# The last four head tiles of branch A in the written order, and merge rows loaded one merge ahead

## The chip, the cores and the metric

The kernel runs on one core of a Trainium2 chip. The core has a matrix engine (TensorE, PE in the profile, with PEld for the loading of its stationary operand), a vector engine (VectorE, DVE), a scalar engine (ScalarE, ACT), a general one (GpSimd, POOL) and a queue that mostly issues transfers (SyncE, SP). Each works through its own instructions in order and waits on semaphores for the others. The metric is the device time of one execution in microseconds (us); less is better.

## The reference, cut to what matters

One encoder layer over 1280 rows (1024 of a sample, 256 of a prompt), width 1024, with two attention branches, gates, an MLP and a final norm:

```python
z = rmsnorm(x, g_mix) @ w_in                 # q, k, v of both branches, and 2 x 1024 gate columns
gates = sigmoid(z[..., o6:] + b_gate)
o_a = banded_attention(qa, ka, va, 128, 1, bias_a, sink)     # 8 heads of 64
o_b = dilated_mixture(qb, kb, vb, bias_b)    # three groups of 4 heads; softmax over the groups' lse
merged = gates[0] * (o_a @ w_branch_a) + gates[1] * (o_b @ w_branch_b)
x = x + merged @ w_out
y = rmsnorm(x + square(relu(rmsnorm(x, g_mlp) @ w_up)) @ w_down, g_final)
```

Matrix products are made from two parts of each operand, a high and a low half (`hi` and `lo`), with three matmuls per product.

## The kernel before, in words

The layer is worked off in stages: input projection and branch B's attention (up to about 600 us), branch A's heads (600 to 768), the branch products with the gates (768 to 860), then `merged @ w_out` and the MLP. The change is in the heads and the branch products.

**The heads.** Branch A has 40 head tiles: four units (two heads each) of ten row tiles. Tile i goes through three steps, in three successive rounds of a loop: `scores` (L1016 to L1024: four score matmuls into two `sc` banks, on DVE a reduction per head, L1018, which also adds the bias, then `nm_a`, L1022, the exponentials on ACT, L1024), `transposes` (L1039: four or six 128x128 transposes on PE into `pt` banks, and their copies), `values_of` (L1053: the value matmuls, a copy, a store to `scr_o`). After each step stands `tick(n)`, n = 0 to 125, which puts other work between: fill and merges.

- Fill is `logits()`: five weight chunks of gate columns times all rows, in 45 steps of eight matmuls (L192), six of them ahead of the loop; `done[0] * 122 < 39 * n` places the others. Their results are stored to `scr_g` (L1076).
- A merge (L1078 to L1122) takes rows of branch B's three groups from `scr_b`, in a tile `r` (loads L1086 to L1097), weighs them by the softmax of their lse on DVE and ACT (L1102 is its first DVE instruction) and leaves `merged`. There are ten, of four steps each, from n = 32 on. The loads are the merge's first step, its arithmetic the next.
- `turn_merged(t)` turns two 128x128 blocks of `merged` on PE (L1137) into one `pt` bank; `split` then writes the high half on ACT (`obhi`, L185) and the low half on DVE (`oblo`, L186), per block.

The bank pools: three `mm`, two `sc`, two `pt`, one `pv`. A `pt` bank is used by a head tile's transposes, by `turn_merged` and by `turn_a`, and comes free when its readers are done.

**The branch products.** 48 jobs of one 128-column chunk and one block of rows each; for the first block eight of branch B (six matmuls), then four of branch A (twelve). A job's product is multiplied by its gate (L1262, L1264) into `mT`. Gates are loaded from `scr_g` (L1222) and opened with the sigmoid (L1227), five and two jobs ahead. A table `side` says before which jobs `turn_a` and `turn_merged` run. `turn_a(t)` divides a row tile of branch A's output by its sum (L1155, DVE), turns its four blocks (L1158, PE) and splits them (`ohi`, `olo`). Weights pass through `fetch` (the load, L222) and `prepare` (`whi` on ACT, L231, `wlo` on DVE, L235).

**What sets the order.** The stages up to 600 us, and from the second half of `w_out` on, are issued in the order in which they are written (`tc.manual_schedule`). In the heads and the branch products a scheduler decides the order of each engine's instructions from the written program.

Of the kernel before, what the change touches and what calls it, by code (L numbers as in the profile page):

```python
# [10 lines left out]
F32 = mybir.dt.float32  # L11
# [4 lines left out]
P = 128  # L16
# [81 lines left out]
def encoder_kernel(  # L98
# [31 lines left out]
    def wslot(name, shape=(P, D), dt=F32):  # L130
        return slots.tile(list(shape), dt, name=name, tag="w", bufs=N_W)
# [52 lines left out]
    def split(hi, lo, src):  # L184
        nc.scalar.activation(hi, src, AF.Copy)  # L185
        nc.vector.tensor_tensor(lo, src, hi.bitcast(F32), op=ALU.subtract)  # L186
# [199 lines left out]
    def then(*gens):  # L386
        for g in gens:
            yield from g
# [604 lines left out]
    if True:  # L993
# [84 lines left out]
        def merge(i, t):  # L1078

            r = wslot("r", (P, 2, 3, ROW))
# [16 lines left out]
            yield  # L1099
            nm, ls = r[:, :, :, 2 * HD : 2 * HD + 2], r[:, :, :, 2 * HD + 2 :]  # L1100
            mm = small.tile([P, 2, 2], F32, name="mm_", tag="m")
            nc.vector.tensor_tensor(mm, nm[:, :, 0], nm[:, :, 1], op=ALU.min)  # L1102
# [20 lines left out]
            yield  # L1123


    mT = Wide("mT", KC, F32, ())
    if True:
        ob_hi, ob_lo = Wide("obhi", 2, F32R, ()), Wide("oblo", 2, F32R, ())
        o_hi, o_lo = Wide("ohi", 4, F32R, ()), Wide("olo", 4, F32R, ())

        def turn_merged(t):
            if t in (0, 4, 8):
                ob_hi.block(t // 4)
                ob_lo.block(t // 4)
            ps = bank("pt")
            for j in range(2):
                nc.tensor.transpose(ps[:, P * j : P * j + P], merged[t // 4][:, t % 4, P * j : P * j + P], ident)  # L1137
            k = 8 if t < 8 else 2
            for j in range(2):
                hi, lo = (x.at(j, P * t, P).rearrange("p (q m) -> p q m", m=k) for x in (ob_hi, ob_lo))  # L1140
                split(hi, lo, ps[:, P * j : P * j + P].rearrange("p (m q) -> p q m", m=k))

        rows_o = {}

        def load_o(t):
            rows_o[t] = slot("o", (P, AH, HD))
            nc.sync.dma_start(rows_o[t], scr_o[t].rearrange("p (h d) -> p h d", h=AH))

        def turn_a(t):
# [5 lines left out]
            nc.vector.tensor_tensor(o, o, l_a[:, :, t].unsqueeze(2).to_broadcast([P, AH, HD]), op=ALU.mult)  # L1155
            ps = bank("pt")
            for k in range(4):
                nc.tensor.transpose(ps[:, P * k : P * k + P],  # L1158
                                    o[:, 2 * k : 2 * k + 2, :].rearrange("p h d -> p (h d)"), ident)
            p3 = ps.rearrange("p (k q) -> p k q", k=4)  # L1160
            per = o_hi.per(P * t)
            for k in range(0, 4, per):
                split(o_hi.at(k, P * t, P, per), o_lo.at(k, P * t, P, per), p3[:, k : k + per, :])
# [5 lines left out]
        merges = then(*[merge(i, t) for t in range(0, NT, 2) for i in range(2)])  # L1169
        done = [0, 0]  # L1170

        def tick(n):
# [12 lines left out]
            while done[1] * 80 < 40 * (n - 32):  # L1185
                next(merges, None)
                done[1] += 1

        steps_of(fill, 6)
        for i in range(len(order) + 2):  # L1190
            if i < len(order):
                u, t = order[i]
                if t == 0 and u < 3:
                    units[u + 1] = load_unit(u + 1), load_bias(u + 1, lambda name, shape: a3(name, shape, 2))
                scores(u, t)
                tick(3 * i)
# [11 lines left out]
        w_as = [weight(0), weight(0), None, None]  # L1208

        jobs = [(x, b, c) for b in range(3) for x in "ba" for c in range(KC if x == "b" else 4)]  # L1210
        jobs += [("a", b, c) for b in range(3) for c in range(4, KC)]
# [14 lines left out]
                c = jobs[i][2] + KC * (jobs[i][0] == "b")  # L1226
                nc.scalar.activation(sgs[i], sgs[i], AF.Sigmoid, bias=bg[:, c : c + 1])  # L1227

        for i in range(5):
            load_gate(i)  # L1230
        open_gate(0)
        open_gate(1)
        side = {0: (turn_a, 0), 2: (turn_merged, 4), 3: (turn_a, 1), 4: (turn_merged, 5), 5: (turn_a, 2),
                6: (turn_merged, 6), 7: (turn_a, 3), 9: (turn_merged, 7), 12: (turn_a, 4), 14: (turn_a, 5),
                16: (turn_a, 6), 18: (turn_a, 7), 20: (turn_merged, 8), 22: (turn_merged, 9), 26: (turn_a, 8),
                30: (turn_a, 9)}
        for i, (x, b, c) in enumerate(jobs):
            t0, n = BLOCKS[b]
            load_gate(i + 5)
            open_gate(i + 2)  # L1240
            if i in side:
                f, t = side[i]
                f(t)
                if f is turn_a and t + 4 < NT:
                    load_o(t + 4)
            if i in (24, 28):
# [494 lines left out]
```

## Time and profile before

| | us |
|---|---|
| runs | 1784.59, 1785.34, 1787.38 |
| median | 1785.34 |
| profiled execution: time | 1786.2 |
| profiled execution: span | 1784.4 |
| PE busy in the span | 1729.1 (97%) |
| DVE, ACT, POOL busy | 988.8, 716.3, 502.1 |

How to read the profile's lines. A timeline row gives the start and the length in us, the engine, the line of the kernel, the operation, output<-inputs, its shape, how many like it, and in brackets the engine's idle time before it with what released it. A row of a group gives the count, then the busy time, the mean in ns, and the idle time before it. A row of waits gives the waiting engine and line, what it waited for, then total, times and the longest. "fp32r" is the type of the split halves. The clock (PEclk) is the share of its full speed that TensorE was granted.

### The profile page before, as it was taken

What the parts mean: (1) busy time and instruction counts of PE and PEld (TensorE: products, weight loads), DVE (VectorE), ACT (ScalarE), POOL (GpSimd) and SP (SyncE); (2) the same over time, 40 slices, a digit from 0 to 9 for tenths busy, and PEclk for the clock granted to TensorE, in tenths of its full rate; (3) what the DMA queues carried; (4) which work ended last, traced back from release to release, by engine and by line L of the source; (5) the groups of instructions that cost most, each with busy time, mean ns of one, the idle gap of its engine ahead of it and who ended that gap; (6) DMA issues with size and microseconds to landing.
All of it is one profiled execution on the core that took longest, in us unless ns stands there. A gap on an engine that the chain in (4) does not pass through costs nothing.

```text
span 1784.4 us, 25203 instructions
## 1 busy us (share of the span) xinstructions
PE 1729.1 (97%) x9248; PEld 1464.8 (82%) x9248; DVE 988.8 (55%) x1683; ACT 716.3 (40%) x1533; POOL 502.1 (28%) x396
## 2 busy tenths in 40 slices
PE   7999999999999999899999799999999999999998
PEld 6898888777777899878888688888888788888886
DVE  6623333355545357676647655454554875667575
ACT  6232223344444354465336433333333433333345
POOL 0222321223222111100010345455555451315050
PEclk9999999999999999999999899999999999999999
DMA  6415335555454833454411144433445854623333
GB/s 231 144 38 165 108 105 148 141 149 147 138 160 144 289 110 100 142 207 158 158 44 80 57 129 151 150 122 125 130 151 175 300 200 144 237 98 121 120 112 118
DMA packets 218067, 256.26 MB, mean 144 GB/s; under 512 B 21455, under 2 KB 148771, under 8 KB 217816
## 3 DMA queue, kind: packets, MB, share of 16 engines
q1 hardware_dynamic: 209512, 232.32, 40.2%
q0 software_dynamic: 7344, 20.24, 3.4%
q10 hardware_dynamic: 1088, 2.10, 0.3%
q8 instruction: 73, 1.20, 0.3%
q14 instruction: 50, 0.41, 0.1%
HBM read 169.10 MB, written 90.73 MB: 146 GB/s over the span
## 4 chain that ended last, share of the span: by engine, by line
PE 61%; DVE 4%; ACT 2%; issue 1%; DMA 1%; SPq 0%; POOL 0%; DVEq 0%; ACTq 0%; POOLq 0%
PE dn L344 20%; PE mm L192 13%; PE x L344 10%; PE pv L344 5%; PE z L344 4%; PE y L344 2%; PE pv L1053 2%; PE pt L1039 1%; PE sc L1016 1%; PE sc L1017 1%; PE mm L344 1%; DVE ulo L186 0%; PE pv L538 0%; DMA scr_u<-u 0%; DVE clo L311 0%
## 5 line engine op out<-in xcount | busy, mean ns | idle before, releaser
L344 PE MATMUL x<-chi,wlo 128*128 128x512 f32 x424 | 171.8, 405 | 6.9 <-ACT phi L185 6.9
L344 PE MATMUL dn<-dhi,ulo 128*128 128x512 f32 x448 | 174.6, 390 | 2.6 <-DVE ulo L186 2.6
L344 PE MATMUL dn<-dhi,uhi 128*128 128x512 f32 x448 | 174.3, 389 | 0.0
L344 PE MATMUL dn<-dlo,uhi 128*128 128x512 f32 x448 | 174.3, 389 | 0.0
L344 PE MATMUL x<-clo,whi 128*128 128x512 f32 x424 | 168.3, 397 | 0.0
L344 PE MATMUL x<-chi,whi 128*128 128x512 f32 x424 | 167.8, 396 | 0.0
L377 POOL TENSOR_TENSOR tb<-raw 128x512 f32<-128x512 f32 x30 | 40.1, 1338 | 442.6 <-PE mm L192 130.0
L311 DVE TENSOR_TENSOR wlo<-ta,whi 128x1024 fp32r<-128x1024 f32 x30 | 55.9, 1864 | 186.3 <-ACT whi L309 171.7
L311 DVE TENSOR_TENSOR wlo<-raw,whi 128x1024 fp32r<-128x1024 f32 x60 | 92.2, 1537 | 106.5 <-ACT whi L309 106.5
L344 PEld LDWEIGHTS dn<-dhi,ulo 128*128 128x128 f32 x448 | 84.1, 188 | 20.9 <-DVE ulo L186 3.6
L344 PEld LDWEIGHTS x<-chi,wlo 128*128 128x128 f32 x424 | 81.7, 193 | 22.9 <-ACT phi L185 7.3
L344 PEld LDWEIGHTS dn<-dhi,uhi 128*128 128x128 f32 x448 | 84.1, 188 | 17.6
L186 DVE TENSOR_TENSOR ulo<-uraw,uhi 128x1024 fp32r<-128x1024 f32 x56 | 91.9, 1662 | 11.7 <-ACT uhi L185 11.7
L344 PEld LDWEIGHTS dn<-dlo,uhi 128*128 128x128 f32 x448 | 84.1, 188 | 17.3
L344 PEld LDWEIGHTS x<-chi,whi 128*128 128x128 f32 x424 | 81.3, 192 | 18.0
L515 ACT ACTIVATE s<-s,o 128x128 f32<-128x128 f32 (+1 forms) x120 | 52.4, 437 | 102.8 <-DVE o L513 55.0
L344 PEld LDWEIGHTS x<-clo,whi 128*128 128x128 f32 x424 | 81.7, 193 | 14.4
L1458 POOL TENSOR_TENSOR t<-raw,t 128x1024 f32<-128x1024 f32 x16 | 47.2, 2969 | 142.5 <-DMA raw<-in_w_down_dram 138.4
L1609 DVE TENSOR_TENSOR v<-v,dn 128x512 f32<-128x512 f32 x90 | 59.5, 682 | 42.5 <-PE dn L344 38.2
L344 PE MATMUL dn<-dhi,up 128*128 128x512 f32 x224 | 73.5, 389 | 0.0
L344 PE MATMUL pv<-phi,wlo 128*128 128x256 f32 x256 | 72.4, 283 | 0.9 <-ACT u L1629 0.9
L344 PE MATMUL z<-chi,wlo 128*128 128x512 f32 x184 | 72.6, 395 | 0.0
(327 smaller groups left out, 4753.2 us busy)
## 6 DMA issues: line engine op xcount, KB each, us to landing
scr_u<-u SPq DMA_DIRECT2D x112, 320.0 KB
uraw<-scr_u SPq DMA_DIRECT2D x56, 512.0 KB
raw<-in_w_in_dram SPq DMA_DIRECT2D x33, 512.0 KB
raw<-in_w_up_dram SPq DMA_DIRECT2D x32, 512.0 KB
raw<-in_w_down_dram SPq DMA_DIRECT2D x28, 512.0 KB
sg<-scr_g SPq DMA_DIRECT2D x32, 256.0 KB
uraw<-scr_u SPq DMA_DIRECT2D x28, 256.0 KB
v<-scr_v SPq DMA_DIRECT2D x96, 64.0 KB
```

Of the source, the lines that this page charges most:

```text
L186: nc.vector.tensor_tensor(lo, src, hi.bitcast(F32), op=ALU.subtract)
L192: nc.tensor.matmul(ps, a, b, start=i == 0, stop=i == len(seq) - 1)
L311: nc.vector.tensor_tensor(lo, src, hi.bitcast(F32), op=ALU.subtract)
L344: nc.tensor.matmul(ps, a, b, start=first and i == 0, stop=last and i == len(seq) - 1, skip_group_check=True)
L377: nc.gpsimd.tensor_tensor(tb[:, 0], b12, b11, op=ALU.subtract)
L515: nc.scalar.activation(s[:, h, :W], s[:, h, :W], AF.Exp, bias=nm[:, h : h + 1], accum_out=l[:, h : h + 1])
L1016: nc.tensor.matmul(ps[:, :W], q, st["k"][1][:, P * lo : P * lo + W], start=True, stop=False)
L1017: nc.tensor.matmul(ps[:, :W], q, st["k"][0][:, P * lo : P * lo + W], start=False, stop=True)
L1039: nc.tensor.transpose(ps[:, P * (i % 4) : P * (i % 4) + P], s[:, h, P * b : P * b + P], ident)
L1053: nc.tensor.matmul(pv[:, HD * h : HD * h + HD], pt[:, 2 * b + h, :], src, start=b == 0, stop=b == W // P - 1)
L1458: nc.gpsimd.tensor_tensor(o, a, b, op=ALU.subtract)
L1609: nc.vector.tensor_tensor(v, v, ps, op=ALU.add)
```

## The change

1. A merge's rows are loaded one merge ahead (`load_rows`, `merges_of`): the loads of the first merge go out before its first step, and those of merge n + 1 ahead of the arithmetic of merge n. Merges begin at n = 6 in place of 32 and run at 41 steps per 96 in place of 40 per 80.
2. Fill runs at 31 steps per 120 in place of 39 per 122, and stops at 31 of the 39. Of the eight left, four run in the last two rounds of the loop, which have no scores, three or four among the divisions of the first row tiles, and the rest behind them.
3. From tile 36 until job 40 the written order holds (`last.enter_context(tc.manual_schedule(engines=ALL))` to `last.close()`).
4. `turn_merged` 0 to 3 stand at the beginning of rounds 36 to 39. The turn leaves the low halves to `low_b`, which stands behind that round's scores. The two weights of branch B are prepared in rounds 38 and 40.
5. All gate loads and sigmoids stand behind the heads' exponentials. Loads are six and sigmoids three jobs ahead.
6. `turn_a` is three steps, `divide`, `turn_a` and `low_a`, placed in a new table; several can stand at one job. Branch A's weights are prepared at jobs 5, 8, 33 and 35.

The core of the diff:

```diff
+        def merges_of(seq):
+            load_rows(*seq[0])
+            for n, x in enumerate(seq):
+                yield
+                if n + 1 < len(seq):
+                    load_rows(*seq[n + 1])
+                yield from merge(*x)
...
         def turn_merged(t):
...
             for j in range(2):
                 hi, lo = (x.at(j, P * t, P).rearrange("p (q m) -> p q m", m=k) for x in (ob_hi, ob_lo))
-                split(hi, lo, ps[:, P * j : P * j + P].rearrange("p (m q) -> p q m", m=k))
+                parts.append((hi, lo, ps[:, P * j : P * j + P].rearrange("p (m q) -> p q m", m=k)))
+            banks_t["b", t] = parts
+            for hi, _, src in parts:
+                nc.scalar.activation(hi, src, AF.Copy)
+
+        def low_b(t):
+            for hi, lo, src in banks_t.pop(("b", t)):
+                nc.vector.tensor_tensor(lo, src, hi.bitcast(F32), op=ALU.subtract)
...
         def tick(n):
 
-            while done[0] * 122 < 39 * n:
+            while done[0] * 120 < 31 * n and done[0] < 31:
                 next(fill, None)
                 done[0] += 1
-            if n in (104, 112):
-                fetch()
-            elif n == 115:
-                prepare()
-            elif n in (106, 109, 113, 117):
-                turn_merged((106, 109, 113, 117).index(n))
-            elif n in (119, 121, 122, 125):
-                load_o((119, 121, 122, 125).index(n))
-            while done[1] * 80 < 40 * (n - 32):
+            while done[1] * 96 < 41 * (n - 6):
                 next(merges, None)
                 done[1] += 1
+            if n in (96, 104):
+                fetch()
 
         steps_of(fill, 6)
         for i in range(len(order) + 2):
+            if i == 36:
+
+                last.enter_context(tc.manual_schedule(engines=ALL))
+            if 36 <= i < 40:
+                turn_merged(i - 36)
+            if i in (38, 40):
+                prepare()
             if i < len(order):
...
                 scores(u, t)
                 tick(3 * i)
+            else:
+                next(fill)
+            if 36 <= i < 40:
+                low_b(i - 36)
             if 0 <= i - 1 < len(order):
                 transposes(*order[i - 1])
                 tick(3 * i + 1)
+            if i >= len(order):
+                next(fill)
             if 0 <= i - 2 < len(order):
                 values_of(*order[i - 2])
                 tick(3 * i + 2)
-        run(fill)
+            if i in (38, 39):
+                load_o(i - 38)
         run(merges)
         sums_a()
...
+        for i in range(4):
+            divide(i)
+            if i < 3:
+                open_gate(i)
+            next(fill)
+        run(fill)
+        load_gate(4)
+        load_gate(5)
+        side = {0: [(turn_a, 0)], 1: [(low_a, 0), (turn_a, 1)], 2: [(low_a, 1), (turn_merged, 4)],
+                3: [(low_b, 4), (turn_a, 2)], 4: [(low_a, 2), (turn_a, 3)], 5: [(low_a, 3), (turn_merged, 5)],
+                6: [(low_b, 5), (turn_merged, 6)], 7: [(low_b, 6), (turn_merged, 7)], 8: [(low_b, 7), (divide, 4)],
...
         for i, (x, b, c) in enumerate(jobs):
             t0, n = BLOCKS[b]
-            load_gate(i + 5)
-            open_gate(i + 2)
+            if i == 40:
+                last.close()
+            load_gate(i + 6)
...
+            for f, t in side.get(i, ()):
                 f(t)
...
+            open_gate(i + 3)
+            if i in (1, 4, 22, 26):
                 fetch()
-            elif i == 33:
-                w_as[2:] = weight(0), weight(0)
+            elif i in (5, 8, 33, 35):
+                w_as[(5, 8, 33, 35).index(i)] = weight(0)
```

How it moves instructions, at three places. DVE before, at the turn of merged tile 0 (its two low halves are the rows `oblo`), where the last merge begins (`mm__` from the loaded rows `r`) and the reductions of head tile 36 follow (`s,m`):

```order
L186 TENSOR_TENSOR oblo_0_7508<-pt,obhi_0_7507 128x128
L1102 TENSOR_TENSOR mm__7534<-r 128x4
L1018 ISA s,m<-sc,bias 128x384
L1018 ISA m 128x1
L1103 TENSOR_TENSOR mm__7534<-mm__7534,r 128x4
L1018 ISA s,m<-sc,bias 128x384
L1018 ISA m 128x1
L186 TENSOR_TENSOR oblo_0_7508<-pt,obhi_0_7507 128x128
```

DVE now, from the reductions of tile 37 to the low halves of merged tile 2:

```order
L1018 ISA s,m<-sc,bias 128x256
L1018 ISA m 128x1
L1022 SCALAR_TENSOR_TENSOR nm_a<-m,nsink 128x2
L1165 TENSOR_TENSOR oblo_0_7476<-pt,obhi_0_7475 128x128 x2
L264 COPY pt<-pt 128x512
L264 COPY o<-pv 128x128
L235 TENSOR_TENSOR wlo<-raw,whi 128x1024
L1018 ISA s,m<-sc,bias 128x256
L1018 ISA m 128x1
L1018 ISA s,m<-sc,bias 128x256
L1018 ISA m 128x1
L1022 SCALAR_TENSOR_TENSOR nm_a<-m,nsink 128x2
```

The two low halves of a merged tile stand together, behind both reductions of the head tile; those of merged tile 2 come next, so behind the weight's low half as well. No instruction of a merge is left here.

PE before, from the turn of merged tile 2 to that of tile 3 (L1137), with the scores, transposes and values of head tiles and eight matmuls of fill and more between:

```order
L1137 MATMUL pt<-ident,merged 128x128 x2
L1016 MATMUL sc<-kp,qp 128x256
L1017 MATMUL sc<-kp,qp 128x256
L1016 MATMUL sc<-kp,qp 128x256
L1017 MATMUL sc<-kp,qp 128x256
L1039 MATMUL pt<-ident,s 128x128 x4
L1053 MATMUL pv<-va,pt 128x64 x6
L192 MATMUL mm<-hhi,whi 128x512
```

PE now, from the turn of merged tile 2 to that of tile 3 (L1153):

```order
L1153 MATMUL pt<-ident,merged 128x128 x2
L1016 MATMUL sc<-kp,qp 128x256
L1017 MATMUL sc<-kp,qp 128x256
L1016 MATMUL sc<-kp,qp 128x256
L1017 MATMUL sc<-kp,qp 128x256
L1039 MATMUL pt<-ident,s 128x128 x4
L1053 MATMUL pv<-va,pt 128x64 x6
L1153 MATMUL pt<-ident,merged 128x128 x2
```

The fill between the two turns is gone; it stands behind the next scores. (A value matmul of this listing is two rows of the trace.)

ACT now, behind the last head tile (before, `ACT_TABLE_LOAD` stood at three places between exponentials and sigmoids):

```order
L1024 ACTIVATE s,l_a<-s,nm_a 128x256 x2
L262 ACTIVATE gs<-mm 128x512
L262 ACTIVATE o<-pv 128x128
L231 ACTIVATE whi<-raw 128x1024
L262 ACTIVATE o<-pv 128x128 x2
L1063 ACTIVATE nm_a<-nm_a 128x80
L1270 ACT_TABLE_LOAD
L1270 ACTIVATE sg<-sg,bg 128x512 x3
L262 ACTIVATE gs<-mm 128x512
```

All exponentials stand ahead of the one table load, and the sigmoids behind it.

More of the change, by code (lines that the diff above doesn't have):

```diff
@@ L1076, in logits, with load_rows @@
                     nc.sync.dma_start(scr_g[c][:, t0 : t0 + n], z[:, :n])
-        def merge(i, t):
-            r = wslot("r", (P, 2, 3, ROW))
+        def load_rows(i, t):
+            r = rows_b[i, t] = wslot("r", (P, 2, 3, ROW))
             for j in range(2):
@@ L1098, in merge @@
                         "(r q) c -> r q c", r=2)[:, 64 * j : 64 * j + 64])
-            yield
+        def merge(i, t):
+            r = rows_b.pop((i, t))
             nm, ls = r[:, :, :, 2 * HD : 2 * HD + 2], r[:, :, :, 2 * HD + 2 :]
@@ L1123, in merge @@
             yield
+        def merges_of(seq):
[5 more added lines that the diff above has]
+                yield from merge(*x)
+        rows_b = {}
     mT = Wide("mT", KC, F32, ())
@@ L1129, in encoder_kernel @@
         o_hi, o_lo = Wide("ohi", 4, F32R, ()), Wide("olo", 4, F32R, ())
+        banks_t = {}
         def turn_merged(t):
@@ L1138, in turn_merged @@
             k = 8 if t < 8 else 2
+            parts = []
             for j in range(2):
                 hi, lo = (x.at(j, P * t, P).rearrange("p (q m) -> p q m", m=k) for x in (ob_hi, ob_lo))
[L1141 removed]
+                parts.append((hi, lo, ps[:, P * j : P * j + P].rearrange("p (m q) -> p q m", m=k)))
[5 more added lines that the diff above has]
+                nc.vector.tensor_tensor(lo, src, hi.bitcast(F32), op=ALU.subtract)
         rows_o = {}
@@ L1147, in load_o, with divide @@
             nc.sync.dma_start(rows_o[t], scr_o[t].rearrange("p (h d) -> p h d", h=AH))
+        def divide(t):
+            o = rows_o[t]
+            nc.vector.tensor_tensor(o, o, l_a[:, :, t].unsqueeze(2).to_broadcast([P, AH, HD]), op=ALU.mult)
         def turn_a(t):
@@ L1161, in turn_a, with low_a @@
             per = o_hi.per(P * t)
-            for k in range(0, 4, per):
-                split(o_hi.at(k, P * t, P, per), o_lo.at(k, P * t, P, per), p3[:, k : k + per, :])
+            parts = [(o_hi.at(k, P * t, P, per), o_lo.at(k, P * t, P, per), p3[:, k : k + per, :])
+                     for k in range(0, 4, per)]
+            banks_t["a", t] = parts
+            for hi, _, src in parts:
+                nc.scalar.activation(hi, src, AF.Copy)
+        def low_a(t):
+            for hi, lo, src in banks_t.pop(("a", t)):
+                nc.vector.tensor_tensor(lo, src, hi.bitcast(F32), op=ALU.subtract)
         load_prompt(0, unit0[0])
@@ L1168, in encoder_kernel @@
         fill = logits()
-        merges = then(*[merge(i, t) for t in range(0, NT, 2) for i in range(2)])
+        merges = merges_of([(i, t) for t in range(0, NT, 2) for i in range(2)])
         done = [0, 0]
+        w_bs = []
+        last = ExitStack()
         def tick(n):
-            while done[0] * 122 < 39 * n:
+            while done[0] * 120 < 31 * n and done[0] < 31:
                 next(fill, None)
                 done[0] += 1
-            if n in (104, 112):
-                fetch()
-            elif n == 115:
-                prepare()
-            elif n in (106, 109, 113, 117):
-                turn_merged((106, 109, 113, 117).index(n))
-            elif n in (119, 121, 122, 125):
-                load_o((119, 121, 122, 125).index(n))
-            while done[1] * 80 < 40 * (n - 32):
+            while done[1] * 96 < 41 * (n - 6):
                 next(merges, None)
                 done[1] += 1
+            if n in (96, 104):
+                fetch()
         steps_of(fill, 6)
         for i in range(len(order) + 2):
+            if i == 36:
[4 more added lines that the diff above has]
+                prepare()
             if i < len(order):
@@ L1207, in encoder_kernel @@
         w_bs = [weight(0), weight(0)]
-        w_as = [weight(0), weight(0), None, None]
+        w_as = [None] * 4
         jobs = [(x, b, c) for b in range(3) for x in "ba" for c in range(KC if x == "b" else 4)]
@@ L1227, in open_gate @@
                 nc.scalar.activation(sgs[i], sgs[i], AF.Sigmoid, bias=bg[:, c : c + 1])
[L1229 to L1236, printed above, removed]
+        load_gate(0)
@@ new lines, in encoder_kernel @@
+        load_gate(1)
+        load_o(2)
+        load_gate(2)
+        load_gate(3)
+        load_o(3)
+        for i in range(4):
[9 more added lines that the diff above has]
+                6: [(low_b, 5), (turn_merged, 6)], 7: [(low_b, 6), (turn_merged, 7)], 8: [(low_b, 7), (divide, 4)],
+                9: [(turn_a, 4), (divide, 5)], 10: [(low_a, 4), (turn_a, 5)], 11: [(low_a, 5), (divide, 6)],
+                13: [(turn_a, 6)], 14: [(low_a, 6), (divide, 7)], 15: [(turn_a, 7)], 16: [(low_a, 7)],
+                17: [(turn_merged, 8)], 18: [(low_b, 8), (turn_merged, 9)], 19: [(low_b, 9), (divide, 8)],
+                20: [(turn_a, 8)], 21: [(low_a, 8), (divide, 9)], 22: [(turn_a, 9)], 23: [(low_a, 9)]}
@@ L1237, in encoder_kernel @@
         for i, (x, b, c) in enumerate(jobs):
             t0, n = BLOCKS[b]
-            load_gate(i + 5)
-            open_gate(i + 2)
-            if i in side:
-                f, t = side[i]
-                f(t)
-                if f is turn_a and t + 4 < NT:
-                    load_o(t + 4)
-            if i in (24, 28):
+            if i == 40:
+                last.close()
+            load_gate(i + 6)
+            if i in (0, 1, 2, 3, 8, 9):
+                load_o(i + 4 if i < 4 else i)
```

1 line of the change is left out of this document (removed).

## The prediction, made before the result was known

> **What bounds the kernel now.** I read the page first, then TensorE's waits in the stretch that the change touches (the head tiles and the branch products, 600 to 862 us), then the stretches around the longest wait, then single rows.
>
> The page:
>
> ```profile
> span 1784.4 us, 25203 instructions
> PE 1729.1 (97%) x9248; PEld 1464.8 (82%) x9248; DVE 988.8 (55%) x1683; ACT 716.3 (40%) x1533; POOL 502.1 (28%) x396
> ```
>
> TensorE (PE) is busy for 97% of the span. The change gives it no matmul more or less, so only two things can move the time: idle time of PE, and its clock. The waits of PE between 600 and 862 us (total, times, longest):
>
> ```profile
> PE pt L1039 <- DVE nm_a L1022: 4.7, 1, 4.7
> PE pt L1158 <- DVE olo L186: 2.2, 1, 2.2
> PE mm L192 <- DVE mlo L186: 1.3, 1, 1.3
> PE pt L1137 <- DVE oblo L186: 1.0, 1, 1.0
> PE pv L1053 <- DVE o L264: 0.5, 1, 0.5
> PE pv L1053 <- ACT o L262: 0.3, 1, 0.3
> PE pt L1039 <- DVE pt L264: 0.3, 1, 0.3
> ```
>
> So about 10 us are all that this stretch can give. The row of 1.3 us stands after the branch products, where the order is not touched. Busy time of PE, its clock and the DMA rate by stretches (start:end length, then PE, PEld, DVE, ACT, POOL, PEclk, DMA share, GB/s):
>
> ```profile
> 744.00:749.00 5.00, 0.26 (x2) 0.20 (x2) 1.64 (x9) 0.44 (x3) 0.54 (x1) 0.98 0.83 266
> 749.00:752.00 3.00, 3.00 (x15) 3.00 (x15) 2.30 (x9) 1.92 (x8) 0.00 (x0) 0.50 0.62 234
> ...
> 780.00:790.00 10.00, 8.98 (x44) 7.33 (x44) 7.63 (x17) 9.16 (x20) 0.00 (x0) 1.00 1.05 390
> ...
> 440.00:443.00 3.00, 3.00 (x8) 1.93 (x9) 0.01 (x1) 0.18 (x1) 0.55 (x1) 0.50 0.71 211
> ```
>
> After the long wait PE runs at half clock for 3 us, which loses 1.5 us more. What the long wait is, DVE's rows show, with PE's:
>
> ```profile
> 741.29 0.29 DVE L186 TENSOR_TENSOR oblo<-pt,obhi 128x128 fp32r<-128x128 f32 x1 [0.43 <-ACT obhi L185]
> 746.23 0.16 DVE L1102 TENSOR_TENSOR mm__7534<-r 128x4 f32<-128x4 f32 x1 [4.65 <-DMA r<-scr_b__82]
> 746.31 0.56 DVE L1018 CUSTOM_DVE_ANT_0 s<-sc,bias 128x384 f32<-128x384 f32 x1
> ...
> 748.40 0.29 DVE L186 TENSOR_TENSOR oblo<-pt,obhi 128x128 fp32r<-128x128 f32 x1
> ```
>
> ```profile
> 748.83 0.66 PE L1039 MATMUL pt<-ident,s 128*128 128x128 f32 x2 [4.74 <-DVE nm_a L1022]
> ```
>
> DVE stood for 4.65 us at the last merge's row, waiting for its load. The second low half of the first turned tile (748.40) was queued behind it and kept one of the two `pt` banks; PE started 0.14 us after it ended. The releaser named, `nm_a`, ran beside it and is not the cause.
>
> **The change part by part.**
>
> *Rows a merge ahead.* Every merge's loads now go out one merge before its first DVE instruction, four merge steps, or about 9 ticks, ahead. The same loads are issued, so SP's own cost is the same, but they now stand ahead of the next unit's key and query loads. PE had no wait for keys or queries in this stretch (none is in its table), so I take 0, with 2 us as the upper bound, the size of its second wait. Removed: 4.74 + 1.5 = 6.2 us.
>
> *Turned rows.* Before, `turn_a` and `turn_merged` sat in DVE's queue where the scheduler put them. Two more waits of PE came from this:
>
> ```profile
> 774.10 0.63 PE L1158 MATMUL pt<-ident,o 128*128 128x128 f32 x4 [2.20 <-DVE olo L186]
> 781.17 0.41 PE L1137 MATMUL pt<-ident,merged 128*128 128x128 f32 x2 [1.02 <-DVE oblo L186]
> ```
>
> Both go with the old order: 3.2 us. With the small rows of the table (0.5 + 0.3 + 0.3 = 1.1), what is removed is 6.2 + 3.2 + 1.1 = 10.5 us.
>
> Now what is late next. In the new order, the low halves of a turned merged tile (`low_b`) are queued on DVE behind the reductions of the head tile that follows. Each holds a bank that PE wants soon. The durations (name, count, total, mean ns):
>
> ```profile
> L1018 DVE CUSTOM_DVE_ANT_0 s<-sc,bias 128x384 f32<-128x384 f32 x48 | 25.5, 552 | 13.2 <-PE sc L1017 12.9
> L1018 DVE CUSTOM_DVE_ANT_0 s<-sc,bias 128x256 f32<-128x256 f32 x32 | 12.7, 421 | 20.4 <-PE sc L1017 16.0 <-ACT s L1024 2.2 <-ACT o L262 2.1
> L1022 DVE SCALAR_TENSOR_TENSOR nm_a<-m,nsink 128x2 f32<-128x2 f32 x40 | 6.3, 157 | 0.2
> L186 DVE TENSOR_TENSOR oblo<-pt,obhi 128x128 fp32r<-128x128 f32 x20 | 5.7, 286 | 3.9 <-ACT obhi L185 3.9
> L185 ACT ACTIVATE obhi<-pt 128x128 fp32r<-128x128 f32 x20 | 5.4, 270 | 5.3 <-PE pt L1137 4.4 <-DVE oblo L186 0.8
> L231 ACT ACTIVATE whi<-raw 128x1024 fp32r<-128x1024 f32 x17 | 17.9, 1052 | 7.1 <-DMA raw<-in_w_in_dram 5.5 <-DMA raw<-in_w_out_dram 1.0 <-DVE wlo L235 0.5
> L235 DVE TENSOR_TENSOR wlo<-raw,whi 128x1024 fp32r<-128x1024 f32 x15 | 18.3, 1218 | 0.5 <-PE mm L192 0.4
> L1262 DVE TENSOR_TENSOR mT<-mm,sg 128x512 f32<-128x512 f32 x16 | 10.9, 686 | 1.9 <-PE mm L192 1.9
> L1227 ACT ACTIVATE sg<-sg,bg 128x512 f32<-128x512 f32 x32 | 21.5, 719 | 1.9 <-DMA sg<-scr_g 1.8
> L1158 PE MATMUL pt<-ident,o 128*128 128x128 f32 x40 | 6.0, 273 | 2.2 <-DVE olo L186 2.2
> ```
>
> And PE's own steps, from one head tile in full flow:
>
> ```profile
> 730.52 0.48 PE L192 MATMUL mm<-hlo,whi 128*128 128x512 f32 x1
> ...
> 732.45 0.34 PE L1016 MATMUL sc<-kk,q 128*128 128x384 f32 x1
> ...
> 733.15 0.82 PE L1039 MATMUL pt<-ident,s 128*128 128x128 f32 x6
> 734.30 1.55 PE L1053 MATMUL pv<-va,pt 128*128 128x64 f32 x12 [0.34 <-ACT o L262]
> 735.66 0.36 PE L192 MATMUL mm<-phi,wlo 128*128 128x256 f32 x1
> ```
>
> From starts to starts: eight matmuls of 512 columns, 1.93 us (0.24 each); four score matmuls, 0.70 (at 256 columns I take 0.70 x 256/384 = 0.47); values, 1.36; four transposes of the six, about 0.5. Handing on between engines: 0.14. DVE's rows overlap by 0.08 (746.23 + 0.16 against 746.31), for which I take a little off each chain.
>
> - At head tile 36, the transposes of tile 35 want the bank of turned tile 0 for their last two. Chain: half the scores 0.35 + 0.14, two reductions 1.10, `nm_a` 0.16, two `oblo` 0.57, 0.14 = 2.46. PE's cover: scores 0.70 + four transposes 0.5 = 1.2. PE waits about 1.2 us.
> - At tile 37, the same with 256 columns: 0.24 + 0.14 + 0.84 + 0.16 + 0.57 + 0.14 = 2.09 against 0.97: 1.0 us.
> - At tile 39, turned tile 3 wants the bank of turned tile 2, whose low halves stand behind a weight's low half (`wlo`), which waits for `whi` on ACT behind `obhi`: 0.14 + 0.54 + 1.05 + 1.22 + 0.84 + 0.16 + 0.57 + 0.14 = 4.66 against 0.47 + 0.5 + 1.36 = 2.33: 2.0 us.
> - At job 7, turned tile 7 wants the bank of tile 5, whose low halves stand behind another `wlo` and job 5's product: 0.14 + 0.54 + sigmoid 0.72 + 1.05 + 1.22 + 0.69 + 0.57 + 0.14 = 5.07 against two jobs of six matmuls and a turn, 2 x 1.45 + 0.2 = 3.1: 1.6 us after the overlaps.
>
> Bounds of these four together: 0, if the durations' overlap and earlier idle cover them; 5.8, as summed; and each row may be followed by a half-clock stretch (below). The four turns of branch A in jobs 0, 1, 3 and 4 just fit: the bank of the first comes back after job 0, its product and two low halves (1.45 + 0.14 + 0.69 + 0.84 = 3.1 us) against two jobs and a turn (3.4); I take 0, up to 1.
>
> *Less fill in the heads.* Of the 39 gate steps left after the first six, 31 run with the 40 tiles where all 39 did. Tiles without fill have their softmax chain less covered. The cover lost is 8 x 1.93 us at most, but it comes back on PE behind the heads, where it covers the sum of the exponentials, the division and the first sigmoids. The small waits of 0.3 and 0.5 us come from this kind of tightness; I take one back: +0.5, from 0 to 2.
>
> *Gates and weights moved.* One table load remains of three, off PE's path: 0. The loads of gate 4 and later, of rows 4 to 9 and of branch A's weights now stand on SP behind the store of the last gate chunk, which waits for the end of the fill. Up to the first weight that is, by the shapes, six loads of 256 KB and one of 512 KB: 2.0 MB, or 5.1 us at the 390 GB/s of 780 to 790. If issue and landing add 3 us, which is assumed, it is there 8 us after the fill. ACT wants it at job 5: five jobs of 1.45, four turns of 0.5, two of 0.2 and 1.4 for `obhi` and a sigmoid, 11 us after. Cost 0; the slack is some 3 us.
>
> *The clock.* A wait need not be long to cost twice:
>
> ```profile
> 438.03 1.84 PE L538 MATMUL pv<-v,pt 128*128 128x64 f32 x8 [2.31 <-issue]
> ```
>
> After this gap of 2.31 us the clock was 0.50 (440 to 443, above), while after the 2.20 us at 774 it stayed at 1.00 (780 to 790). A half-clock stretch of 3 us costs 1.5 us. My waits are below both gaps, so I add none. The Trainium skill (TensorE: Matmul & The Clock Gate, Part 1) has the clock fall after at least one idle window of about 3.4 us; by that rule no wait here would lower it, and the sum would be the one below; by the row at 438, where a shorter gap did, the wait of 2.0 us may add 1.5. The trace does not agree with the rule as a lower limit.
>
> Sum: -10.5 + 5.8 + 0.5 = -4.2 us. The profiled execution took 1786.2 us (1784.4 span, 1.8 around it) and would take 1782.0; the median of the runs, 0.9 us lower at 1785.34, becomes 1781.1.
>
> **The rivals.**
>
> *The low halves' waits are hidden.* If DVE is ahead of PE (the reductions overlap, ACT is early), two or more of the four waits vanish: 1785.34 - 10.5 + 2 to 0.5 = 1775 to 1777. For it: DVE is only 55% busy. Against it: the chains begin at PE's own instructions, so no engine can be ahead of them.
>
> *The waits move and bring the clock with them.* Four waits within some 30 us, each with a half-clock stretch: -4.2 + 4 x 1.5 = +1.8, so 1787.1; with one or two, 1782.6 to 1784.1, no change that can be measured. For it: the row at 438. Against it: 2.20 and 1.02 us within 8 us around 774 to 781 left the clock at 1.00. The Trainium skill's section on a second failure of the clock (same page, PSUM-queue depth-cycling) would have frequent short idles make the clock oscillate, which is this rival.
>
> *The loads are late (slower).* The loads behind the fill's last store make ACT wait for the weight at job 5; `obhi` of tile 6 and `wlo`, the products and the low halves are queued behind, and PE stops with all its banks taken. Each us past the slack is a us of PE. To end slower by 3.57 us it takes 3.57 + 4.2 = 7.8 us of stop (6.3 with one half-clock stretch), that is the 2.0 MB in 5.1 + 3 + 7.8 = 15.9 us, or 126 GB/s. For it: the same burst was there at 780 to 790, with the DMA full (1.05). Against it: it moved 390 GB/s. The time is then 1788.9, and a stop of 10 us gives 1791.
>
> **How the numbers follow.** What can be told from no change is 0.2%, 3.57 us. My forecast, 1781.1 with its own range 1779 to 1783.3, has 0.45; it lies close to the bound (1781.8), so two thirds of that, 0.30, count as faster and 0.15 as the same. Hidden waits 0.15, faster. Clock and waits that give it all back 0.21, the same. Late loads, or another stop of that size, 0.19, slower. Faster 0.45, same 0.36, slower 0.19. The range 1776 to 1791 leaves out about 0.05 below and 0.12 above.
>
> **What would show it.** After: no wait of DVE for a merge's row near the end of the heads and no half clock there; PE's waits at the head transposes L1039 and at L1153 released by `oblo` (L1165), 1 to 2 us each, four in number; none above 0.5 us at L1185; one table load between heads and products. I am wrong if PE waits for sigmoids or for products in the first ten jobs, if a wait for keys or queries appears at units 1 to 3, or if the clock drops after the short waits.

## The result and the profile after

The change makes the kernel slower. Over seven runs of each (the three of the table ahead are among those of the kernel before) the median went from 1787.38 to 1790.83 us, 3.45 us more. The ratio on record is 1.0026, with a 95% interval of 1.0017 to 1.0035, which is some 4.6 us. Either is the wrong way: 4.2 us were forecast as gain. The profiled executions differ by 4.4 us in span, 1784.4 against 1788.8.

```profile
span 1788.8 us, 25229 instructions
PE 1731.5 (97%) x9248; PEld 1466.8 (82%) x9248; DVE 991.7 (55%) x1683; ACT 714.1 (40%) x1531; POOL 501.6 (28%) x396
```

TensorE's waits from 595 to 872 us in the changed kernel (waiting engine and line, what it waited for, then total, times, longest):

```profile
PE pt L1153 <- DVE oblo L1165: 4.2, 2, 2.3
PE pt L1039 <- ACT s L1024: 3.6, 1, 3.6
PE pt L1039 <- DVE oblo L1165: 2.0, 2, 1.1
PE pt L1185 <- DVE o L1176: 1.4, 2, 0.8
PE mm L192 <- DVE mlo L186: 1.3, 1, 1.3
```

Apart from the row of 1.3 us behind the products, all that was there before has gone: no wait for a merge's row, none of 2.2 us at a turn of branch A. Two of the new ones were forecast, the low halves (`oblo`). Two were not: 3.6 us for exponentials and 1.4 us for divisions.

TensorE's single rows with their places, and the stretches behind the two waits after which the clock fell (length; busy time of PE, PEld, DVE, ACT, POOL; clock; DMA share and rate):

```profile
629.88 1.04 PE L1039 MATMUL pt<-ident,s 128*128 128x128 f32 x4 [3.56 <-ACT s L1024]
...
737.46 0.41 PE L1039 MATMUL pt<-ident,s 128*128 128x128 f32 x2 [1.14 <-DVE oblo L1165]
743.02 0.41 PE L1039 MATMUL pt<-ident,s 128*128 128x128 f32 x2 [0.89 <-DVE oblo L1165]
750.96 0.41 PE L1153 MATMUL pt<-ident,merged 128*128 128x128 f32 x2 [1.91 <-DVE oblo L1165]
783.97 0.66 PE L1153 MATMUL pt<-ident,merged 128*128 128x128 f32 x2 [2.30 <-DVE oblo L1165]
804.43 0.63 PE L1185 MATMUL pt<-ident,o 128*128 128x128 f32 x4 [0.85 <-DVE o L1176]
812.88 0.63 PE L1185 MATMUL pt<-ident,o 128*128 128x128 f32 x4 [0.51 <-DVE o L1176]
```

```profile
630.00:633.50 3.50, 3.50 (x15) 3.31 (x16) 1.69 (x8) 1.54 (x5) 0.38 (x1) 0.51 0.22 65
...
784.00:790.00 6.00, 6.00 (x23) 4.88 (x24) 3.61 (x9) 2.73 (x5) 0.00 (x0) 0.75 1.04 382
```

Lost time in the changed kernel, between the heads' first scores and the last branch product: waits of 3.56 + 1.14 + 0.89 + 1.91 + 2.30 + 0.85 + 0.51 = 11.2 us, and half clock worth 3.5 x 0.49 + 6.0 x 0.25 = 3.2 us; together 14.4. Before it was 9.2 us of waits (the table in the prediction without its row of 1.3 us, and 0.2 us for `olo`) and 1.7 us of half clock (3.41 us at 0.50 from 748.75 on, of which the prediction's view shows three): 10.9. The difference is +3.5 us.

That agrees with the length of the stretch itself. It is measured here from the start of the heads' first score matmul (L1016) to the start of the first matmul behind the products (the one that waits 1.31 us for `mlo` in every trace): 602.75 to 861.35 before, 603.55 to 865.52 after.

| kernel | span, us | the stretch, us | ratio of times to the kernel before, 95% interval |
|---|---|---|---|
| before | 1784.4 | 258.6 | |
| changed | 1788.8 | 262.0 | 1.0026 (1.0017 to 1.0035) |
| merges from tick 16 | 1785.5 | 258.4 | 0.9991 (0.9981 to 1.0001) |
| low halves ahead of the scores | 1784.2 | 257.1 | 1.0002 (0.9990 to 1.0015) |
| low half of tile 5 at job 5 | 1787.1 | 263.1 | 1.0010 (0.9998 to 1.0021) |
| the three edits above and two divisions | 1773.5 | 249.2 | 0.9943 (0.9927 to 0.9960) |
| before, rows ahead | 1776.4 | 252.5 | 0.9966 (0.9953 to 0.9978) |
| before, rows ahead, merges from tick 6 | 1782.3 | 255.7 | 0.9977 (0.9967 to 0.9986) |
| changed, second fill weight fetched first | 1782.5 | 258.3 | 1.0005 (0.9995 to 1.0015) |
| all edits, no written order | 1772.2 | 246.3 | 0.9932 (0.9920 to 0.9945) |
| changed, no written order | 1778.3 | 251.4 | 0.9961 (0.9947 to 0.9974) |

What lies ahead of the stretch and behind it is the same work in all kernels, and yet differs by up to 2.4 us on either side. So the stretch, and the waits in it, tell more than the span.

**Where the 3.56 us come from.** ScalarE and the queue of SyncE (SPq) at that place:

```profile
628.17 1.06 ACT L231 ACTIVATE whi<-raw 128x1024 fp32r<-128x1024 f32 x1 [4.51 <-DMA raw<-in_w_in_dram]
629.13 0.60 ACT L1024 ACTIVATE s<-s,nm_a 128x384 f32<-128x384 f32 x1
```

```profile
609.78 0.72 SPq L1086 DMA_DIRECT2D r<-scr_b__81  x1
...
619.46 0.58 SPq L1091 DMA_DIRECT2D r<-scr_b__83  x1
620.13 0.40 SPq L1076 DMA_DIRECT2D scr_g<-gs  x1
620.58 0.43 SPq L222 DMA_DIRECT2D raw<-in_w_in_dram  x1
```

ScalarE stood for 4.51 us before the second fill weight's high half, and the exponentials of a head tile are queued behind it. The weight's load was issued at 620.58, behind the row loads of the first two merges: sixteen of them, from 609.78 to 620.04, some 0.6 us each. In the kernel before, the same rows read:

```profile
612.69 0.39 SPq L222 DMA_DIRECT2D raw<-in_w_in_dram  x1
```

```profile
617.36 1.06 ACT L231 ACTIVATE whi<-raw 128x1024 fp32r<-128x1024 f32 x1 [1.65 <-DMA raw<-in_w_in_dram]
```

There the load went out 7.9 us earlier, and the high half waited for it 1.65 us even so, without stopping TensorE. ScalarE had no slack left before the change. The load is also slower: from its issue to the high half 7.6 us pass in the changed kernel and 4.7 before (7.0 to 7.9 in the five traces with the rows ahead of it, 4.5 to 5.3 in the five in which they are not and the high half waits for it). So of the 10.8 us by which the high half comes later, 7.9 are the later issue and 2.9 a later arrival. What makes the arrival later, the bytes of the rows ahead of it or the other loads beside it, no run separates.

### The profile page after: what moved, and what is told of

Same layout as the page of the kernel before. It is cut to its first block, busy times and chain, and to the rows that moved or that the text cites. A ratio compares the mean times of both kernels' runs of the same rounds, so it can differ in the third digit from the quotient of the medians.

```text
span 1788.8 us, 25229 instructions
## 1 busy us (share of the span) xinstructions
PE 1731.5 (97%) x9248; PEld 1466.8 (82%) x9248; DVE 991.7 (55%) x1683; ACT 714.1 (40%) x1531; POOL 501.6 (28%) x396
## 4 chain that ended last, share of the span: by engine, by line
PE 61%; DVE 3%; ACT 2%; DMA 2%; issue 1%; POOL 0%; SPq 0%; ACTq 0%; DVEq 0%; POOLq 0%
PE dn L344 20%; PE mm L192 13%; PE x L344 10%; PE pv L344 5%; PE z L344 5%; PE y L344 2%; PE pv L1053 2%; PE pt L1039 1%; PE sc L1016 1%; PE sc L1017 1%; PE mm L344 1%; DMA raw<-in_w_down_dram 0%; DVE ulo L186 0%; PE pv L538 0%; DMA raw<-in_w_in_dram 0%
```

## The experiments

Theory A: the time is lost at places in queues. The fill weight's load stands behind row loads on SP; low halves and divisions stand behind other work on DVE; each is worth its wait, and the parts add up. The rivals are named with each run. Each ratio is to runs of the kernel before in the same session.

### Merges begin at tick 16

```diff
-            while done[1] * 96 < 41 * (n - 6):
+            while done[1] * 86 < 41 * (n - 16):
```

> The changed kernel with one number changed: merges begin at tick 16 (41 steps per 86) in place of tick 6. Theory A: the 3.56 us wait near 626 us is the second fill weight, whose load is issued behind 16 row loads on SP; the weight is now issued ahead of them, so that wait and the half-clock stretch behind it (1.7 us) go: about -5.2 us, a span of 1783.6 against 1788.8, ratio to the kernel before 0.9996. Rival B: the load is late because transfers or tile slots are scarce in this stretch, whoever is first on SP; then a wait of 2 us or more for a fill weight or for keys shows at another place, and the time stays within 1.5 us of the changed kernel, ratio 1.0015 or more.

Measured: 0.9991 (0.9981 to 1.0001); the stretch is 3.6 us shorter than in the changed kernel. TensorE's waits, 595 to 872 us:

```profile
PE pt L1153 <- DVE oblo L1165: 4.5, 2, 2.6
PE pt L1039 <- DVE oblo L1165: 2.0, 2, 1.1
PE pt L1185 <- DVE o L1176: 1.4, 2, 0.8
```

The wait for exponentials is gone, and no wait of TensorE for another weight, for keys or for queries has come: theory A. The stretch shrank by the wait alone, and not by 5.2 us, because in this execution half clock followed the wait of 1.91 us at turned tile 3, where it had not in the changed kernel (last section says why).

### Low halves directly behind the turn, in the heads

```diff
             if 36 <= i < 40:
                 turn_merged(i - 36)
+                low_b(i - 36)
             if i in (38, 40):
                 prepare()
...
-            if 36 <= i < 40:
-                low_b(i - 36)
```

> The changed kernel with the low halves of a merged tile directly behind its turn, ahead of the scores and of the weight's preparation. Theory A: the waits of 1.14, 0.89 and 1.91 us in the heads (PE for oblo, L1165) come from the queue position alone; they shrink to 0.5 us or less together: about -3.4 us, a span of 1785.4. Rival B: the reductions then stand behind obhi, exponentials come later, and PE waits for exponentials or transposes instead: the time stays within 1 us of 1788.8 in span.

Measured: 1.0002 (0.9990 to 1.0015); the stretch is 4.8 us shorter. Waits:

```profile
PE pt L1039 <- ACT s L1024: 3.0, 1, 3.0
PE pt L1153 <- DVE oblo L1165: 2.3, 1, 2.3
PE pt L1185 <- DVE o L1176: 1.4, 2, 0.8
...
PE sc L1016 <- DVE m L1018: 0.7, 1, 0.7
PE pt L1039 <- DVE oblo L1165: 0.2, 1, 0.2
```

Of 1.14 + 0.89 + 1.91 = 3.94 us, 0.2 are left, and 0.7 of a new kind has come: the reductions, now behind the weight's low half, give up a `sc` bank late. The net of 3.0 us is close to the 3.4 of theory A. The place in DVE's queue was the cause. The other 1.8 us of the stretch are not this edit's plan: the wait for exponentials is 0.5 us shorter here, and no half clock followed the wait of 2.29 us at job 7 (1.5 us).

### The low half of tile 5 at job 5

```diff
-                ... 5: [(low_a, 3), (turn_merged, 5)],
-                6: [(low_b, 5), (turn_merged, 6)], ...
+                ... 5: [(low_a, 3), (turn_merged, 5), (low_b, 5)],
+                6: [(turn_merged, 6)], ...
```

> The changed kernel with the low halves of merged tile 5 at job 5, ahead of the weight's preparation on DVE, in place of job 6. Theory A: the 2.30 us wait at job 7 goes, and with it the half-clock stretch of 784 to 790 us (1.5 us): about -3.8 us, a span of 1785.0. Rival B: only the wait goes and another takes its place at job 8, where the weight is wanted (2 us or more there); or the half clock comes anyway: -1 us or less.

Measured: 1.0010 (0.9998 to 1.0021), against 1.0026. Waits:

```profile
PE pt L1039 <- ACT s L1024: 3.4, 1, 3.4
PE pt L1185 <- DVE o L1176: 2.0, 3, 0.8
PE pt L1039 <- DVE oblo L1165: 2.0, 2, 1.1
PE pt L1153 <- DVE oblo L1165: 1.9, 1, 1.9
...
PE mm L192 <- DVE mT L1319: 0.6, 1, 0.6
```

The wait of 2.30 us and its half clock are gone, as theory A said. 0.6 us at a product and 0.6 us more at a division have come in their place, as the rival said, but smaller. Yet the stretch of this execution is 1.1 us longer, since half clock lasted longer near 628 us (9.5 us at 0.64, which is 3.4 us lost, against 1.7) and followed the 1.91 us too:

```profile
627.50:637.00 9.50, 8.66 (x42) 7.89 (x42) 4.18 (x17) 4.19 (x13) 0.54 (x1) 0.64 0.26 80
```

The single trace misleads here; over twelve runs the median is 1787.64 us, against 1786.43 for the kernel before in the same session. The interval still overlaps that of the changed kernel, so the runs alone don't prove the gain; that the wait went is what the trace shows.

### All three edits, and two divisions earlier

```diff
-                13: [(turn_a, 6)], 14: [(low_a, 6), (divide, 7)], 15: [(turn_a, 7)], ...
-                17: [(turn_merged, 8)], ... 19: [(low_b, 9), (divide, 8)],
+                13: [(turn_a, 6), (divide, 7)], 14: [(low_a, 6)], 15: [(turn_a, 7)], ...
+                17: [(turn_merged, 8), (divide, 8)], ... 19: [(low_b, 9)],
```

> The three edits of the first three runs together, and the divisions of row tiles 7 and 8 one and two jobs earlier (these cost 0.85 and 0.51 us). Theory A: the parts add up, -5.2 - 3.4 - 3.8 - 1.4 = -13.8 us, a span of 1775.0 and a ratio to the kernel before of 0.995. Rival B: where waits are closed the next ones open, as PE is fed by the same chains: less than -8 us, a span above 1780.8 and a ratio of 0.998 or more.

Measured: 0.9943 (0.9927 to 0.9960), span 1773.5 against 1775.0 expected. Waits:

```profile
PE mm L192 <- DVE mlo L186: 1.3, 1, 1.3
PE pt L1185 <- DVE o L1176: 0.8, 1, 0.8
PE sc L1016 <- DVE m L1018: 0.7, 1, 0.7
PE pt L1039 <- DVE oblo L1165: 0.2, 1, 0.2
```

The parts add up. The stretch is 12.8 us shorter than in the changed kernel, and no half clock is left in it: 9.5 us of waits and 3.2 of half clock make 12.7. Both division waits of the changed kernel are gone; the 0.8 us is a new one, at the turn of row tile 5 (780.33 us), as the rival said, but small. The two earlier divisions were not run alone.

### The kernel before with rows a merge ahead, alone

```diff
+        def merges_of(seq): ...           # load_rows of the next merge ahead of each merge
-        merges = then(*[merge(i, t) for t in range(0, NT, 2) for i in range(2)])
+        merges = merges_of([(i, t) for t in range(0, NT, 2) for i in range(2)])
```

> The kernel before, in which only the merge's rows are loaded one merge ahead (start and pace of the merges as before, order left to the scheduler). Theory A: DVE no longer stands at the last merge's row, so the wait of 4.74 us and its half-clock stretch (1.5 us) go: -6.2 us, a span of 1778.2 and a ratio to the kernel before of 0.9965. Rival B: the scheduler sorts the freed instructions anew and other waits of together 3 us or more come in the heads: a ratio of 0.998 or more.

Measured: 0.9966 (0.9953 to 0.9978); the stretch is 6.1 us shorter. Waits:

```profile
PE pt L1171 <- DVE olo L186: 2.6, 1, 2.6
PE mm L192 <- DVE mlo L186: 1.3, 1, 1.3
PE pt L1039 <- ACT s L1024: 1.0, 2, 0.9
```

The wait of 4.74 us is gone, as theory A said. This one part of the change would have made the kernel faster by 0.34%. That the 6.1 us are so close to the 6.2 expected is luck: the half clock did not go, it now follows the wait of 2.6 us (from 767.75 us on). In its place 2.1 us of smaller waits went and 1.4 came, and some 0.7 us of the stretch are not accounted for.

### The same with merges from tick 6

```diff
-            while done[1] * 80 < 40 * (n - 32):
+            while done[1] * 96 < 41 * (n - 6):
```

> As the run with rows ahead in the kernel before, with the merges also begun at tick 6 (41 steps per 96). Theory A: the 16 row loads go ahead of the second fill weight on SP here too, so a wait of about 3.5 us and a half-clock stretch (1.6 us) come near 626 us: some 5 us more than with rows ahead alone, a ratio to the kernel before of 0.999 to 1.000. Rival B: that wait belongs to the thinner fill of the changed kernel: it is not there, and the ratio is that of rows ahead alone, 0.9965.

Measured: 0.9977 (0.9967 to 0.9986), between the two expectations. Waits, and ScalarE's row at the second fill weight:

```profile
PE pt L1171 <- DVE olo L186: 2.6, 1, 2.6
PE pt L1039 <- ACT s L1024: 2.0, 3, 1.6
```

```profile
626.12 1.06 ACT L231 ACTIVATE whi<-raw 128x1024 fp32r<-128x1024 f32 x1 [4.86 <-DMA raw<-in_w_in_dram]
```

ScalarE waits as long for the weight as in the changed kernel (4.86 against 4.51 us), but TensorE only 1.85 us (1.58 and 0.27) in place of 3.56; half clock followed (628.54 us). So theory A has the cause right. The fill runs at 39 steps per 122 here, and more matmuls may have stood ready; that the thinner fill of the rival makes up the difference in size is argued, as no run changes the fill alone.

### The second fill weight fetched ahead of the rows

```diff
         steps_of(fill, 6)
+        fetch()
         for i in range(len(order) + 2):
```

> The changed kernel, merges at tick 6 as they are, with one load written earlier: the second fill weight's, ahead of the loop over the head tiles and so ahead of all row loads on SP. Theory A: the wait of 3.56 us near 626 us and its half clock go with the load's place alone: -5.2 us, a span of 1783.6, a ratio to the kernel before of 0.9996. Rival B: early merges cost by themselves (their arithmetic on DVE, their traffic): a wait of 2 us or more stays before 660 us, a ratio of 1.0015 or more.

Measured: 1.0005 (0.9995 to 1.0015); the stretch is 3.6 us shorter than in the changed kernel. Merges still begin at tick 6. Waits:

```profile
PE pt L1153 <- DVE oblo L1165: 4.4, 2, 2.5
PE pt L1039 <- DVE oblo L1165: 2.0, 2, 1.1
PE pt L1185 <- DVE o L1176: 1.4, 2, 0.8
```

No wait is left near 626 us. The place of one load on SP was the cause of that wait, not the early merges by themselves. The stretch shrank by 3.6 and not by 5.2 us, since half clock followed the wait of 1.91 us here too. Whether early merges cost something besides is not settled: with late ones the ratio was 0.9991, and the two intervals overlap.

### The changed kernel without the written order

```diff
             if i == 36:
-                last.enter_context(tc.manual_schedule(engines=ALL))
+                pass
```

> The changed kernel without the written order from tile 36 to job 40: the scheduler decides, all else as changed. Theory A (the waits in the heads and jobs belong to the written order): the scheduler places the weight's low half ahead of the four turns and divisions earlier, so of 1.14 + 0.89 + 1.91 + 2.30 + 1.36 us at most 2.5 us are left, while the wait of 3.56 us near 626 us and its half clock stay: a span of 1780 to 1783, a ratio to the kernel before of 0.996 to 0.999. Rival B (they belong to the steps being apart, low halves later than turns): the scheduler keeps them behind the reductions, 5 us or more of waits stay, and the ratio is 1.001 or more.

Measured: 0.9961 (0.9947 to 0.9974), span 1778.3. All waits of TensorE in 595 to 872 us:

```profile
PE pt L1039 <- ACT s L1024: 3.5, 1, 3.5
PE mm L192 <- DVE mlo L186: 1.3, 1, 1.3
```

The six waits behind low halves and divisions are gone, all 7.6 us of them. In the scheduler's order the low halves of the first merged tile still stand behind the reductions. But four matmuls of fill or the value matmuls stand between the first four transposes of a head tile and the last two, which want the bank, where the written order had all six in a row; and the low half of branch B's first weight is ahead of all four turns. The divisions are early: all ten are done by 784 us, where the changed kernel has the last two at 803.60 and 812.05. The stretch is 10.5 us shorter; 7.6 us of waits and 1.5 us of half clock make 9.1, and 1.4 us are not accounted for. From 1.0026 to 0.9961: the written order, as it was written here, costs 0.65%, more than the 0.39% that all else in the change gains.

### All edits, without the written order

The version with all edits, and in it:

```diff
             if i == 36:
-                last.enter_context(tc.manual_schedule(engines=ALL))
+                pass
```

> The version with all edits, without the written order from tile 36 to job 40: the scheduler decides as it did before. Theory A: what counts is where the instructions stand, and the scheduler mixes low halves and divisions with other work again: waits of 2 to 4 us in all come back, a span of 1775.5 to 1777.5 against 1773.5. Rival B: the written order itself gives nothing: within 1 us of 1773.5, with less than 1.5 us of new waits.

Measured: 0.9932 (0.9920 to 0.9945), the fastest kernel of this study, span 1772.2. The only wait left in 595 to 872 us is the one behind the products:

```profile
PE mm L192 <- DVE mlo L186: 1.3, 1, 1.3
```

Theory A expected waits of 2 to 4 us to come back; none did. The rival was right, though the span is 1.3 us lower and it allowed 1: with loads and low halves in good places, the written order gives nothing. Between 0.9943 and 0.9932 the intervals overlap.

## Why the prediction was wrong, point by point

- **What would be removed (-10.5 us): right.** All the waits named went, 4.74 us and its half clock among them. Rows ahead alone took 6.1 us off the stretch where the prediction had 6.2, but there the half clock only moved to another wait, so that agreement is luck.
- **Low halves in the heads (1.2, 1.0 and 2.0 us): right**, with 1.14, 0.89 and 1.91 measured, at the places named.
- **Low halves at job 7 (1.6 us): mechanism right, 2.30 measured.** ACT waited for the gate of the sigmoid that the chain has ahead of the weight:

```profile
779.89 0.72 ACT L1270 ACTIVATE sg<-sg,bg 128x512 f32<-128x512 f32 x1 [0.87 <-DMA sg<-scr_g]
```

  The chain had 0 for that load. The rival of late loads named it as a danger of many us; it came, but as 0.87 us.
- **The step that failed: "Rows a merge ahead", costed at 0 with 2 us as the upper bound.** It said that the row loads stand ahead of keys and queries on SP, and looked for a wait of PE there. It did not name the fill weight's load, which stands behind them in the same queue, and it dealt with the earlier start of the merges not at all. Sixteen loads of about 0.6 us each moved it by 7.9 us, and it took 2.9 us longer to arrive. The trace of before held both numbers, the issue at 612.69 and the wait of 1.65 us that `whi` already had. It cost 3.56 us and 1.7 of half clock.
- **The clock, "I add none": wrong.** It fell behind the 2.30 us at job 7, where the prediction's 1.6 was thought to be too short (1.5 us), and behind the 3.56 us that was not foreseen (1.7 us). Comparing the length of a wait with that of other waits was the wrong test (last section). That the 1.91 us in the heads brought none in the profiled execution is luck: in three other traces they did.
- **"*Less fill in the heads*", +0.5: wrong in kind.** No small wait came. The thin fill may have made the wait for the weight longer (1.85 and 3.56 us in two kernels in which the load is late); these differ in more than the fill, so this is not shown.
- **Branch A's turns in the first jobs, 0: right. Later divisions: not looked at.** The divisions of row tiles 7 and 8 stand in the job before their turn; 0.85 and 0.51 us.

In sum: -4.2 + 3.56 + 1.7 + 1.5 (half clock at job 7) + 0.7 (job 7) + 1.36 (divisions) - 0.3 (heads) - 0.5 (fill) = +3.8 us, against +3.4 in the stretch. The range just held the result (its end is 1791, the median 1790.83), but not for its reason; the sign was wrong, for the likeliest case lacked a stop that none of the rivals had at its right place. "Another stop of that size" had its share of the 0.19 for slower, without a place.

## What to carry to other kernels

When a load is moved earlier, list every load that is then behind it in the same queue, with its issue time and how long its user waits already, weights included: a queue that took 0.6 us for each of these loads is a resource like an engine. An order written by hand is worth what its places are worth; a low half or a division belongs directly behind what it needs, ahead of what waits for something else, or the scheduler does better. And undo one part at a time: of this change one part alone gained 0.34%, and its written order lost 0.65%.

## What the runs showed of the hardware that was not expected

The same wait is followed by half clock in one execution and not in another. The wait of 1.91 us at turned tile 3 is in four traces with the same length; behind it the clock was (changed kernel, then merges from tick 16):

```profile
751.00:754.50 3.50, 3.50 (x24) 3.12 (x24) 1.69 (x9) 2.93 (x11) 0.54 (x1) 1.00 0.06 19
```

```profile
745.50:749.00 3.50, 3.40 (x12) 2.92 (x13) 1.57 (x8) 3.07 (x12) 0.54 (x1) 0.58 0.06 19
```

It fell in three of the four. Waits of 2.2 to 2.6 us in the jobs were followed by half clock in five of seven traces, the wait of some 3.2 us near 980 (all kernels have it) in eight of eleven, that of 6.9 us in all eleven, and the one of 1.31 us behind the products in none of eleven. Each fall lasts some 3.4 us (a few twice that) and loses about 1.7. Falls explain a good part of the spread between runs of one kernel: of 29 runs of the kernel before in one session, the nine with a granted clock of 0.991 have a mean span of 1782.6 us, the three with 0.986 one of 1788.9.

The clock records of the traces tell more than the lengths. In each trace all falls stand on one grid of 3.413 us: those of the kernel before at 438.14, 748.75 and 987.69 us, for example, are 91 and 70 steps apart. What counts is the idle time of TensorE within one step of the grid. Between 595 and 1700 us in all eleven traces, the clock fell behind each of the 33 steps at full clock with 1.85 us or more of it, and behind none with 1.78 or less (ahead of 595 us also behind some with 1.35 to 1.7). The 1.91 us of the changed kernel lay across a grid point at 749.47, 0.42 us ahead of it and 1.49 behind; with merges from tick 16 all of it, 743.69 to 745.60, lay in one step. So did the 2.31 us at 438 from which the prediction argued, while its 2.20 us at 774 were split into 0.75 and 1.45.

The Trainium skill (TensorE: Matmul & The Clock Gate, Part 1) calls the activity window free-running, which agrees with the grid; its idle bound of about 3.4 us does not, since 1.85 us in one step were enough here. Where a wait will lie on the grid is not known ahead of a run. So a wait of more than about 1.8 us has a chance of costing 1.7 us more, and a sum should carry it as a chance. By an estimate from the step of 3.41 us and a bound of 1.8 us, the chance is about a half for 1.9 us, six in ten for 2.3 and nine in ten for 3.2.
